# Two tiles of a depthwise convolution as block Toeplitz products on TensorE, and kept weights without their high halves, in a two-layer decoder trunk in fp32

## The chip, the cores and the metric

The kernel runs on one core of one Trainium2 chip. The metric is the device time of one launch in microseconds (us); lower is better. The engines of the core are TensorE (PE, with its weight loads listed apart as PEld), VectorE (DVE), ScalarE (ACT), GpSimd (POOL) and SyncE (SP). In this kernel SP issues the transfers from DRAM and the writes to it, and POOL issues those that read back what the kernel itself has put into DRAM. Each engine works through its own list of instructions in order, and an instruction that waits holds up all that stand behind it in that list.

## The reference

The input x is 512 positions (SEQ) by 1024 channels (D), fp32. There are two layers. Layer 0 mixes by a state-space group and a stick-breaking attention group, layer 1 by a convolution module; behind each mixer stands a feed-forward part with 4096 hidden values, and after each of the four parts a layer norm of 1.414 x + part.

```python
def conformer_conv(x, w_pw1, b_pw1, w_dw, b_dw, ln_g, ln_b, w_pw2, b_pw2):
    h = x @ w_pw1 + b_pw1
    val, gate = jnp.split(h, 2, axis=-1)
    h = val * jax.nn.sigmoid(gate)
    h = lax.conv_general_dilated(
        h, w_dw[:, None, :], window_strides=(1,), padding=[(CONV_SIZE - 1, 0)],
        dimension_numbers=('NWC', 'WIO', 'NWC'), feature_group_count=CONV_WIDTH) + b_dw
    h = jax.nn.silu(layer_norm(h, ln_g, ln_b))
    return h @ w_pw2 + b_pw2

def sqrelu_mlp(x, w1, b1, w2, b2):
    return jnp.square(jax.nn.relu(x @ w1 + b1)) @ w2 + b2
```

The change lies in the convolution module and in what is prepared for it. There each of the 1024 channels is convolved on its own with 31 taps (CONV_SIZE), over the present position and the 30 before it.

## The kernel before

**Products.** Activations lie with channels on the 128 partitions and the 512 positions along the free axis. A fp32 operand is split into a high part in a shorter format (fp32r) and the low rest; a product is then three passes of TensorE: high by high, high by low, low by high (`gemm`, L219). The split is one copy on ACT and one subtraction on DVE (`split`, L215 and L216). Every engine works in the order of its own list; a scheduler at build time makes those lists from the order in which the program names the work and from estimated times, so that neighbours on one engine may come from different loops.

**Weights** (class, L56). Work on weights comes in units of 128 by 1024 values. A unit is fetched by SP into one of two raw buffers, ACT casts it to the high half (L101), DVE subtracts to get the low half (L102), and both go to one of eight slots. A unit is prepared five (or four) units ahead of its use (`AHEAD`), in the order of one list. Thirty units that belong to layer 1 (the list `later`: 16 for the convolution's input projection, `pw1`; 8 for its output projection, `pw2`; 6 for the start of the second feed-forward part) are prepared during the feed-forward part of layer 0, written to DRAM as both halves (`keep`, L109), and read back by POOL when their turn comes (L88).

**Stages, in the order of time.** The mixer of layer 0 comes first; then its output projection and layer norm; then the feed-forward part of layer 0 in four blocks, each of eight hidden tiles `f` (`ffn1`, L988: product, relu, square, split) and the second product `acf` that adds them to X; then the last block's second product with the layer norm folded in, which also begins the next projection on the first half of the positions (`Tail` and `Lead`, tiles `tlb` and `pl`); then the convolution stage; then its output projection `tld`; the second feed-forward part (`fl`, `f`, `g`, `h`); the end.

**The convolution stage** goes over eight tiles of 128 channels. For tile j, `glu_tile` (L1045) makes the value `pv` and the gate `pg` on PE, the sigmoid `csg` of the gate on ACT, the gated product `hp` on DVE with 30 zeros ahead of it, and the split of `hp` into `hph` and `hpl`. The first `PE_TAPS[0][j]` of the 31 taps go to PE (`taps_pe`, L1065): a tap is a product with a diagonal matrix of that tap's weights, in three passes; the matrices `dh` and `dl` are built by ACT from the identity into six buffers (`DBUFS`). Two more taps open the accumulators `cy` and `cz` on ACT, and the rest are multiply-and-add steps on DVE (`taps_dve`, L1078), which end with the addition of `cz` and of PE's `cv`. The sum `sc` over the eight tiles (`LN.add`, L866) is what the layer norm's mean `mpc` is computed from. In the loop at L1095 tile j+2's gate, tile j+1's taps on PE and tile j's taps on DVE are named in turn. The last two tiles are worked in two halves of 256 positions, with taps on PE by `PE_TAPS[1][j]` for the second half, in the order that a string gives:

```python
PE_TAPS = ((2, 6, 8, 9, 11, 14, 13, 14), (10, 10, 10, 10, 10, 10, 13, 8))
TAIL = "P60 P70 V60 V70 G61 G71 N0 P71 P61 V61 V71 N1".split()
```

P is taps on PE, V taps on DVE, G the gate of a second half, N the layer norm of a half; the first digit is the tile, the second the half.

## Time and profile before

| | us |
|---|---|
| median of three runs | 1217.46 (1216.93 to 1217.9) |
| the profiled execution | 1217.5 |
| its span in the profile | 1215.8 |
| granted TensorE clock, mean over the span | 0.995 |
| PE busy | 1187.4 |
| DVE busy | 786.9 |
| ACT busy | 557.1 |
| POOL busy | 58.2 |

The span runs from the first to the last instruction in the profile; the run's time holds 1.7 us more. Times in the timelines are microseconds from the span's start. A row of a timeline gives the start, the length, the engine, the source line with the operation, output and inputs by the names above, and, in brackets, how long the engine was idle before and which instruction released it. A row of groups gives the count, the summed busy time, the mean in ns, and the idle time before these instructions with what ended it. The convolution stage lies between about 662 us (the first gated product) and 795 us (the start of the output projection); the feed-forward part of layer 0 lies ahead of it, from 317 to 594 us.

### The profile page before, as it was taken

What the parts mean: (1) busy time and instruction counts of PE and PEld (TensorE: products, weight loads), DVE (VectorE), ACT (ScalarE), POOL (GpSimd) and SP (SyncE); (2) the same over time, 40 slices, a digit from 0 to 9 for tenths busy, and PEclk for the clock granted to TensorE, in tenths of its full rate; (3) what the DMA queues carried; (4) which work ended last, traced back from release to release, by engine and by line L of the source; (5) the groups of instructions that cost most, each with busy time, mean ns of one, the idle gap of its engine ahead of it and who ended that gap; (6) DMA issues with size and microseconds to landing.
All of it is one profiled execution on the core that took longest, in us unless ns stands there. A gap on an engine that the chain in (4) does not pass through costs nothing.

```text
span 1215.8 us, 16751 instructions
## 1 busy us (share of the span) xinstructions
PE 1187.4 (98%) x6546; PEld 1007.5 (83%) x6546; DVE 786.9 (65%) x1400; ACT 557.1 (46%) x990; POOL 58.2 (5%) x125
## 2 busy tenths in 40 slices
PE   9899999999999999999999999899999999999997
PEld 7677776789988888888999888889988888888885
DVE  7998774578745635646566999998843443434446
ACT  6836665734525524425323456964651332323230
POOL 1001101100000000000022110102000000000000
PEclk9999999999999999999999999999999999999999
DMA  8510042150878787887454631406142232323211
GB/s 205 155 49 22 19 130 61 31 195 1 264 250 282 251 284 264 270 283 268 165 183 159 213 104 36 139 1 208 39 152 87 87 108 83 122 70 121 70 52 69
DMA packets 128943, 168.86 MB, mean 139 GB/s; under 512 B 11298, under 2 KB 101666, under 8 KB 128864
## 3 DMA queue, kind: packets, MB, share of 16 engines
q1 hardware_dynamic: 120064, 136.30, 34.5%
q0 software_dynamic: 8640, 31.46, 7.6%
q8 instruction: 51, 0.84, 0.3%
q14 instruction: 28, 0.23, 0.1%
q10 hardware_dynamic: 160, 0.03, 0.0%
HBM read 132.12 MB, written 35.65 MB: 138 GB/s over the span
## 4 chain that ended last, share of the span: by engine, by line
PE 83%; DVE 10%; ACT 4%; DMA 2%; issue 1%; POOL 0%; SPq 0%; DVEq 0%; POOLq 0%; ACTq 0%
PE f L225 23%; PE g L1175 12%; PE acf L225 11%; PE fl L225 5%; PE tld L225 4%; PE tlb L225 4%; PE h L1159 3%; PE cv L1076 2%; PE pv L225 2%; PE pg L225 2%; PE tla L225 2%; PE pl L225 2%; DVE cz L357 1%; PE acmo L225 1%; PE av L709 1%
## 5 line engine op out<-in xcount | busy, mean ns | idle before, releaser
L102 DVE TENSOR_TENSOR wlo<-raw,whi 128x1024 fp32r<-128x1024 f32 x176 | 213.4, 1224 | 199.5 <-ACT whi L101 198.7
L101 ACT CAST whi<-raw 128x1024 fp32r<-128x1024 f32 x176 | 182.1, 1049 | 313.5 <-PE g L1175 107.4
L1175 PE MATMUL g<-whi,hh 128*128 128x512 f32 x208 | 81.8, 393 | 0.0
L1175 PE MATMUL g<-wlo,hh 128*128 128x512 f32 x208 | 81.8, 393 | 0.0
L1175 PE MATMUL g<-whi,hl 128*128 128x512 f32 x208 | 81.7, 393 | 0.0
L225 PE MATMUL f<-xah,whi 128*128 128x512 f32 x208 | 81.2, 390 | 0.0
L225 PE MATMUL f<-xdl,whi 128*128 128x512 f32 x208 | 81.1, 390 | 0.0
L225 PE MATMUL f<-xah,wlo 128*128 128x512 f32 x208 | 81.0, 390 | 0.0
L225 PE MATMUL f<-xdh,whi 128*128 128x512 f32 x208 | 81.0, 390 | 0.0
L225 PE MATMUL f<-xal,whi 128*128 128x512 f32 x208 | 81.0, 390 | 0.0
L225 PE MATMUL f<-xdh,wlo 128*128 128x512 f32 x208 | 81.0, 390 | 0.0
L225 PE MATMUL acf<-hl,whi 128*128 128x512 f32 x192 | 75.7, 394 | 0.0
L225 PE MATMUL acf<-hh,wlo 128*128 128x512 f32 x192 | 75.6, 394 | 0.0
L225 PE MATMUL acf<-hh,whi 128*128 128x512 f32 x192 | 75.5, 393 | 0.0
L215 ACT CAST hh<-fr 128x512 fp32r<-128x512 f32 x64 | 39.7, 621 | 59.6 <-DVE fr L353 59.6
L216 DVE TENSOR_TENSOR hl<-fr,hh 128x512 fp32r<-128x512 f32 x64 | 44.1, 690 | 31.9 <-ACT hh L215 31.8
L357 DVE SCALAR_TENSOR_TENSOR cy<-hp,wdw,cy 128x512 f32<-128x512 f32 (+1 forms) x99 | 63.6, 654 | 0.2
L357 DVE SCALAR_TENSOR_TENSOR cz<-hp,wdw,cz 128x512 f32<-128x512 f32 (+1 forms) x93 | 60.0, 656 | 0.0
L353 DVE TENSOR_TENSOR fr<-fr 128x512 f32<-128x512 f32 x64 | 43.7, 685 | 14.7 <-ACT fr L154 14.6
L1175 PEld LDWEIGHTS g<-wlo,hh 128*128 128x128 f32 x208 | 39.1, 188 | 8.9
L1175 PEld LDWEIGHTS g<-whi,hl 128*128 128x128 f32 x208 | 39.1, 188 | 8.9
L1175 PEld LDWEIGHTS g<-whi,hh 128*128 128x128 f32 x208 | 39.1, 188 | 8.8
(684 smaller groups left out, 3093.4 us busy)
## 6 DMA issues: line engine op xcount, KB each, us to landing
raw<-in_ffn_w_dram SPq DMA_DIRECT2D x48, 1024.0 KB, 5.8
raw<-in_ffn_w_dram SPq DMA_DIRECT2D x32, 512.0 KB, 3.5
kepth<-whi SPq DMA_DIRECT2D x30, 512.0 KB, 8.6
keptl<-wlo SPq DMA_DIRECT2D x30, 512.0 KB, 9.4
whi<-kepth POOLq DMA_DIRECT2D x30, 512.0 KB, 3.7
wlo<-keptl POOLq DMA_DIRECT2D x30, 512.0 KB, 4.5
raw<-in_conv_w_pw_dram SPq DMA_DIRECT2D x12, 1024.0 KB, 6.5
raw<-in_mix_w_in_dram SPq DMA_DIRECT2D x16, 512.0 KB, 3.9
```

The costliest lines, as they stand in the source:

```text
L101: i0 = nc.scalar.copy(hi, raw).ins
L102: i1 = nc.vector.tensor_sub(lo, raw, hi.bitcast(F32)).ins
L215: i0 = S.copy(hi, src).ins
L216: i1 = V.tensor_sub(lo, src, hi.bitcast(F32)).ins
L225: ins = PE.matmul(ps[:, c0:c1], u[:, k, ksl], v[:, c0:c1], start=start and k == 0 and i == 0, stop=stop and k == n - 1 and i == 2).ins
L353: V.tensor_tensor(o, x, y, op=op)
L357: V.scalar_tensor_tensor(o, x, s, y, op0=op0, op1=op1)
L709: ins = PE.matmul(av[R, P * kb :], vt[:, kb, R], ws_[f"{c}{h}"][0][:, o : o + T - P * kb], start=summed[h] == 1, stop=summed[h] == 4, skip ...
L1076: PE.matmul(cps[j][:, c0:c1], u, v[:, t + c0 : t + c1], start=t == 0 and i == 0, stop=t == n - 1 and i == 2)
L1159: PE.matmul(ps, u, v, start=k == 0 and i == 0, stop=k == nk - 1 and i == 2)
L1175: PE.matmul(pss[b], u, v[:, kk, :], start=k + kk == 0 and i == 0, stop=k + kk == nb - 1 and i == 2)
```

## The change

**Two tiles as Toeplitz products.** Tiles 2 and 3 (`ON_PE`) do their 31 taps on PE alone, in another layout. The 512 positions are taken as four phases (position modulo 4) of 128, and a group of 32 channels with its four phases fills the 128 partitions. An output phase at one shift of whole steps of four positions is then a product with a 128 by 128 matrix that mixes the four phases of a channel. Nine shifts (`SHIFTS`) cover the 31 taps, and there are four groups, so that a tile takes 36 matrices. Each is used in two products (`toeplitz`): the high matrix by the high and the low input side by side, 256 columns, and the low matrix by the high input, 128 columns. `away` adds the two column halves.

The gated product of these tiles is written by phase on DVE (`by_phase`), sent to DRAM and read back in the new layout, then split (`split_phases`); the result goes to DRAM and back (`away`), and ACT puts it into the old order with the bias (`back`). The matrices are made in the feed-forward part of layer 0 (`matrices`): small gathers from a padded copy of the taps, and 36 products of 128 by 512 with a mask on DVE, each written to DRAM by SP. In the convolution stage they are read by POOL into four of the eight weight slots (`M`).

**Kept weights.** Of the thirty kept units only the first four (`BOTH`) are stored as both halves. Of the other 26 the low half is stored; the unit is fetched again by SP and cast again by ACT for the high half, and the low half is read by POOL. The first twenty kept units use four slots only.

**Order and split of taps.** Tiles 1, 4, 5, 6 and 7 have fewer taps on PE for full width and first halves, and tile 7 one fewer in its second half. The order of the first six tiles is written as a string (`CONV_ORDER`: g gate, p taps on PE, v a third of a tile's taps on DVE, s split, m Toeplitz products, o and f the way back, x the scaling of X), and TAIL is another. The buffers of the diagonal matrices go from six to three, the taps are read in the first block rather than ahead of the second, and all additions of `LN.add` are on DVE.

The core of the diff ("..." where lines are left out):

```diff
-PE_TAPS = ((2, 6, 8, 9, 11, 14, 13, 14), (10, 10, 10, 10, 10, 10, 13, 8))
-TAIL = "P60 P70 V60 V70 G61 G71 N0 P71 P61 V61 V71 N1".split()
-DBUFS = 6
+PE_TAPS = ((2, 2, 8, 9, 3, 12, 10, 4), (10, 10, 10, 10, 10, 10, 13, 7))
+TAIL = "G61 P70 P60 V60 V70 G71 N0 P71 P61 V61 V71 N1".split()
+DBUFS = 3
...
+ON_PE = (2, 3)
+SHIFTS = 9
+GROUP = 32
+PARTS = 3
+BOTH = 4
+PAIRS = 1
+CONV_ORDER = "g0 g1 p0 v0 g2 s2 p1 v0 v1 g3 v1 v0 v1 x0 g4 m2 s3 p4 v4 v4 g5 v4 o2 m3 o3 g6 v5 p5 v5 f3 g7 v5 f2".split()
...
+            elif back:
+                i0 = i1 = nc.scalar.copy(hi, raw).ins
+                nc.gpsimd.dma_start(lo, self.kept[back[0]][1])
...
-        for x, d in zip(w, self.kept[i]):
+        for x, d in zip(w, self.kept[i]) if i < BOTH else ((w[1], self.kept[i][1]),):
             self.nc.sync.dma_start(d, x.bitcast(F32))
...
+            if layer == 0 and m >= 8:
+                next(making, None)
...
+    def matrices(i):
...
+        for p_ in range(4):
+            for g in range(4):
+                nc.sync.dma_start(wr[32 * p_ : 32 * p_ + 32, NU * g : NU * (g + 1)], Wd[32 * g : 32 * g + 32, i, p_ : p_ + NU])
+        V.tensor_copy(wh, wr)
+        V.tensor_sub(wl, wr, wh.bitcast(F32))
+        for u in range(0, 4 * NU, 16):
+            for x, src in enumerate((wh.bitcast(F32), wl)):
+                m = tmp(f"m{j}{x}{u}", F32R)
+                V.tensor_tensor(m.rearrange("p (u c) -> p u c", c=GROUP), src[:, u : u + 16].unsqueeze(2).broadcast_to([P, 16, GROUP]),
+                                mask.unsqueeze(1).broadcast_to([P, 16, GROUP]), op=ALU.mult)
+                nc.sync.dma_start(made[j][x][:, u * GROUP : (u + 16) * GROUP], m.bitcast(F32))
+            yield
...
+    def by_phase(j, vps, sg):
...
+        stt(hp[:, :, 8:], ph(vps), pv("conv_b_pw1", j), ph(sg), ALU.add, ALU.mult)
+        Hd = tc.dram_tile([P, 4, P + 8], F32, name=f"Hd{j}")
+        nc.sync.dma_start(Hd, hp)
...
+        for p_ in range(4):
+            nc.sync.dma_start(hps[j][32 * p_ : 32 * p_ + 32], hv[p_])
...
+    def toeplitz(j):
...
+        for g in range(4):
+            o = cps[j][g // 2][:, (g % 2) * 2 * P : (g % 2 + 1) * 2 * P]
+            for e in range(SHIFTS):
+                n = SHIFTS * g + e
+                if n % 8 == 0:
+                    w = M.next()
+                mh, ml = (x[:, n % 8] for x in w)
+                PE.matmul(o, mh, h2[:, :, g, e : e + P], start=e == 0, stop=False)
+                PE.matmul(o[:, :P], ml, h2[:, 0, g, e : e + P], start=False, stop=e == SHIFTS - 1)
+
+    def away(j):
...
+            S.copy(q, z[:, :, 1])
+            tt(r[:, 2 * i * P : (2 * i + 2) * P].rearrange("r (g m) -> r g m", g=2), z[:, :, 0], q, ALU.add)
...
+        nc.sync.dma_start(Od, r.rearrange("r (g m) -> r g m", g=4))
...
+        for g in range(4):
+            nc.sync.dma_start(zv[32 * g : 32 * g + 32], ov[g])
...
-    glu_tile(0)
-    glu_tile(1)
-    taps_pe(0)
-    for j in range(n):
...
+    for o in CONV_ORDER:
```

**How the instructions move, at three places.** The first is ACT's list around the sigmoid of tile 2, `csg` with 512 columns, which the gated product of tile 2 on DVE needs. Before, a diagonal build, the copy for tile 1 (`hph`) and an opened accumulator (`cy`) stand ahead of it:

```order
L154 ACTIVATE dh_6404<-ident,wdh 128x128
L154 ACTIVATE dl_6405<-ident,wdl 128x128
L215 CAST hph_6266<-hp_6265 128x542
L154 ACTIVATE cy_6568<-hp_6265,PV,wdw 128x512
L160 ACTIVATE csg_6362<-pg_6310,PV 128x512
```

Now:

```order
L174 ACTIVATE dl_6863<-ident,wdl 128x128
L235 CAST hph_6406<-hp_6405 128x542
L174 ACTIVATE cy_6555<-hp_6405,PV,wdw 128x512
L174 ACTIVATE cz_6430<-hp_6395,wdw 128x512
L117 CAST whi_6452<-raw_6450 128x1024
L117 CAST whi_6458<-raw_6456 128x1024
L180 ACTIVATE csg_6517<-pg_6467,PV 128x512
```

Two casts of weights (`whi`, for later gates) and one more opened accumulator stand ahead of the sigmoid.

The second place is DVE's list at the end of the convolution stage, where the last addition to `sc` completes the first half's sum (`sc` with 256 columns), and the gated products of the second halves are made (`hp` with 256 columns). Before:

```order
L357 SCALAR_TENSOR_TENSOR hp_6948<-pv_6946,PV,csg_7504 128x256
L353 TENSOR_TENSOR cy_7434<-cy_7434,cz_7435 128x256
L357 SCALAR_TENSOR_TENSOR hp_7140<-pv_7138,PV,csg_7557 128x256
L353 TENSOR_TENSOR cy_7434<-cy_7434,cv_7312 128x256
L216 TENSOR_TENSOR hpl_6950<-hp_6948,hph_6949 128x256
L871 TENSOR_TENSOR sc_6605<-sc_6605,cy_7434 128x256
L216 TENSOR_TENSOR hpl_7142<-hp_7140,hph_7141 128x256
```

Now:

```order
L377 SCALAR_TENSOR_TENSOR cy_7531<-hp_7278,wdw,cy_7531 128x256
L377 SCALAR_TENSOR_TENSOR hp_7278<-pv_7276,PV,csg_7611 128x256
L373 TENSOR_TENSOR cy_7531<-cy_7531,cz_7532 128x256
L373 TENSOR_TENSOR cy_7531<-cy_7531,cv_7405 128x256
L236 TENSOR_TENSOR hpl_7280<-hp_7278,hph_7279 128x256
L373 TENSOR_TENSOR sc_6671<-sc_6671,cy_7531 128x256
```

Tile 6's gated product is earlier in the list, and the low split of tile 7's second half (`hpl_7280`) now stands ahead of the last addition to `sc`, not behind it.

The third is DVE's list at the end of the second block `f` of the feed-forward part of layer 0: `fr` is the square of a hidden tile, `hl` its low split, `X` the first addition of the second product, and `wlo` the low half of a weight unit. Before:

```order
L353 TENSOR_TENSOR fr_4112<-fr_4112 128x512
L102 TENSOR_TENSOR wlo_4208<-raw_4205,whi_4207 128x1024
L102 TENSOR_TENSOR wlo_4238<-raw_4205,whi_4237 128x1024
L216 TENSOR_TENSOR hl_4116<-fr_4112,hh_4115 128x512
L102 TENSOR_TENSOR wlo_4176<-raw_4165,whi_4175 128x1024
L353 TENSOR_TENSOR fr_4150<-fr_4150 128x512
L216 TENSOR_TENSOR hl_4154<-fr_4150,hh_4153 128x512
L353 TENSOR_TENSOR X_61<-X_61,acf_4179 128x512
```

Now:

```order
L373 TENSOR_TENSOR fr_4178<-fr_4178 128x512
L1092 TENSOR_TENSOR m_4188<-w_3891,mask 128x512
L236 TENSOR_TENSOR hl_4182<-fr_4178,hh_4181 128x512
L121 TENSOR_TENSOR wlo_4239<-raw_4236,whi_4238 128x1024
L1092 TENSOR_TENSOR m_4245<-w4h_3892,mask 128x512
L1092 TENSOR_TENSOR m_4248<-w_3891,mask 128x512
L373 TENSOR_TENSOR fr_4222<-fr_4222 128x512
L121 TENSOR_TENSOR wlo_4252<-raw_4236,whi_4251 128x1024
L236 TENSOR_TENSOR hl_4226<-fr_4222,hh_4225 128x512
L373 TENSOR_TENSOR X_61<-X_61,acf_4255 128x512
```

Mask products (`m`) stand among the squares and splits of the hidden tiles, two of them ahead of the last square.

More of the change, by code (lines that the diff above doesn't have):

```diff
@@ L67, in fetch @@
     def fetch(self, i):
[L68 removed]
+        key, src, nk, ncol, off, width, *back = self.units[i]
         if key not in self.chunk:
@@ L832 @@
         if layer:
-            units += [(("split", i), None, 8, 128, 0, 0) for i in range(24 + LEAD)]
+            units += [((f"{u[0][0]}b", *u[0][1:]), *u[1:], i) for i, u in enumerate(later)]
         k0 = 0
@@ L991, in ffn1 @@
             m = k0 + i
+            if then and i == len(first):
+                then()
             if i < len(first):
@@ L1037 @@
         k0 += nb
+    for _ in making:
+        pass
     xs, first = tail_norm_lead(hs, "b", rb[1], ("ln2_g", 0), ("ln2_b", 0), 4, "pl")
+    M.slots = [W.slots[(W.base + 4 + i) % 8] for i in range(4)]
     acc = [None] * KT
@@ L1065, in taps_pe, with back @@
+    def back(j):
+        acc[j] = page(f"cy{j}", F32), None
+        y, zv = acc[j][0].rearrange("c (n q) -> c q n", q=4), cps[j].rearrange("c (q m) -> c q m", q=4)
+        for q in range(4):
+            act(y[:, 3 - q], zv[:, q], AF.Identity, bias=pv("conv_b_dw", j))
     def taps_pe(j, c0=0, c1=T):
```

152 lines of the change are left out of this document (111 added, 41 removed).

## Prediction, made before the changed kernel was run

> **What bounds the kernel now.** I read the page first: the span, and how busy each engine is in it.
>
> ```profile
> span 1215.8 us, 16751 instructions
> PE 1187.4 (98%) x6546; PEld 1007.5 (83%) x6546; DVE 786.9 (65%) x1400; ACT 557.1 (46%) x990; POOL 58.2 (5%) x125
> ```
>
> TensorE (PE) is busy for 98% of 1215.8 us, so it bounds the whole. The one stage where that share misleads is the one changed. The next view gives busy time by stretch of the conv stage (us, PE busy (number of instructions), PEld, DVE, ACT, POOL, granted clock, DMA share, GB/s).
>
> ```profile
> 667.00:700.00 33.00, 33.00 (x146) 27.14 (x146) 32.84 (x52) 14.72 (x37) 5.31 (x10) 1.00 0.62 215
> 700.00:741.00 41.00, 41.00 (x201) 34.50 (x201) 40.51 (x68) 24.87 (x63) 4.22 (x8) 1.00 0.31 103
> 741.00:760.00 19.00, 19.00 (x121) 17.13 (x120) 18.64 (x33) 11.86 (x36) 0.00 (x0) 1.00 0.01 2
> 760.00:783.00 23.00, 18.95 (x156) 18.64 (x154) 23.00 (x55) 21.07 (x65) 4.22 (x8) 1.00 0.54 181
> 783.00:795.00 12.00, 10.30 (x54) 8.84 (x53) 11.62 (x33) 11.20 (x32) 0.00 (x0) 0.86 0.02 6
> ```
>
> VectorE (DVE) is full from 667 to 783 while PE idles for 4 us in the last stretch: two engines run at the edge together, and DVE ends later. The timelines show where (start, length in us, idle before in brackets): first DVE, then PE.
>
> ```profile
> 662.78 0.75 DVE L357 SCALAR_TENSOR_TENSOR hp<-pl,PV,csg 128x512 f32<-128x512 f32 x1 [1.93 <-ACT csg L160]
> 664.24 0.72 DVE L216 TENSOR_TENSOR hpl<-hp,hph 128x542 fp32r<-128x542 f32 x1 [0.71 <-ACT hph L215]
> ...
> 680.83 0.75 DVE L357 SCALAR_TENSOR_TENSOR hp<-pv,PV,csg 128x512 f32<-128x512 f32 x1
> 681.49 0.74 DVE L357 SCALAR_TENSOR_TENSOR cy<-hp,wdw,cy 128x512 f32<-128x512 f32 x1
> ...
> 702.71 0.68 DVE L353 TENSOR_TENSOR cy<-cy,cv 128x512 f32<-128x512 f32 x1
> 703.31 0.74 DVE L357 SCALAR_TENSOR_TENSOR cz<-hp,wdw,cz 128x512 f32<-128x512 f32 x1
> ...
> 778.25 0.50 DVE L357 SCALAR_TENSOR_TENSOR cy<-hp,wdw,cy 128x256 f32<-128x256 f32 x1
> 778.65 0.50 DVE L357 SCALAR_TENSOR_TENSOR cz<-hp,wdw,cz 128x256 f32<-128x256 f32 x1
> ...
> 782.80 0.44 DVE L871 TENSOR_TENSOR sc<-sc,cy 128x256 f32<-128x256 f32 x1
> 783.14 0.44 DVE L216 TENSOR_TENSOR hpl<-hp,hph 128x256 fp32r<-128x256 f32 x1
> ```
>
> ```profile
> 778.36 0.28 PE L225 MATMUL pg<-xbl,whi 128*128 128x256 f32 x1
> 778.48 0.28 PE L225 MATMUL pg<-xbh,wlo 128*128 128x256 f32 x1
> 782.81 0.39 PE L1076 MATMUL cv<-hph,dh 128*128 128x256 f32 x1 [4.05 <-ACT hph L215]
> 783.30 1.22 PE L879 MATMUL mpc<-sc,ones 128*128 128x256 f32 x2
> ```
>
> Durations overlap, so I price by the distance of starts: a 512-wide tap 0.66 us (680.83 to 681.49, both of that operation), a 256-wide tap 0.40, a 512-wide add 0.60 (702.71 to 703.31), a 256-wide add 0.34. The stage on DVE runs from tile 0's gated product (662.78) to the last add of the mean's sum (782.80 + 0.34 = 783.14), 120.4 us; its listed work at these prices is 118.1 (by the order of instructions 130 x 0.66 + 37 x 0.40 + 12 x 0.60 + 18 x 0.34, and 4.2 for splits), so 2.3 are waits. The mean's product (783.30) follows at once, and the output projection starts 12.3 us after the sum:
>
> ```profile
> 655.23 12.00 PE pl L225 x96
> ...
> 700.22 5.49 PE pv L225 x24
> ...
> 795.48 5.46 PE tld L225 x42
> ```
>
> This chain gives PE's prices: 12.00/96 = 0.125 us for a 256-wide product (0.12 between the starts at 778.36 and 778.48 above; I take 0.12), 5.49/24 = 0.229 for a 512-wide one.
>
> **The change, part by part.** *PE.* Removed are 31 full-width taps (tiles 1 to 5: 4+8+9+8+2) of three products, 31 x 3 x 0.229 = 21.3 us, and 14 half-width ones, 14 x 3 x 0.12 = 5.0. Added are 144 Toeplitz products, 72 of 256 columns and 72 of 128, each with its own weight load. A 256-wide product costs 0.12. For 128 columns the trace has few rows (attention scores, 64 rows deep):
>
> ```profile
> 119.38 0.22 PE L672 MATMUL z1B<-qh,kh 64*128 64x128 f32 x1
> 119.44 0.27 PE L672 MATMUL z1B<-ql,kh 64*128 64x128 f32 x1
> 119.55 0.27 PE L672 MATMUL z1B<-qh,kl 64*128 64x128 f32 x1
> ```
>
> Starts lie 0.06 and 0.11 us apart. Bounds of a pair are thus 0.18 and 0.24; I take 0.24, since every product here is behind a load of its own as in the second gap: 72 x 0.24 = 17.3 us. PE's sum: 17.3 - 26.3 = -9.0, of which -8.6 lie ahead of the mean (one half tap of tile 7 comes later). With 0.18 it would be -13.3.
>
> The Trainium skill's "TensorE: Matmul & The Clock Gate" (Back-to-back issue gap) gives about 81 ns per matmul for 128 columns in a stream of load and product. By it a pair is 0.20 and PE's sum -11.9; the rows above hold both readings.
>
> *DVE, conv stage.* Between the same two points the changed list holds 103 instead of 130 operations of 512 (27 x 0.66 = -17.9 us), 50 instead of 37 of 256 taps (+5.2), four 512-wide adds fewer (-2.4) and four 256-wide ones more (+1.4); splits are equal in number. Sum -13.7: with the old waits the sum would end at 769.4. The strided gated product of tiles 2 and 3 is priced as the plain one.
>
> *New waits there.* ACT's builds of diagonal weights (dh), copies, casts and sigmoids cost this much:
>
> ```profile
> L154 ACT ACTIVATE dh<-ident,wdh 128x128 fp32r<-128x128 f32 x98 | 38.3, 391 | 9.2 <-PE cv L1076 6.3 <-DVE wdh L1027 2.8
> L215 ACT CAST hph<-hp 128x542 fp32r<-128x542 f32 x6 | 3.8, 638 | 1.7 <-DVE hp L357 1.7
> L101 ACT CAST whi<-raw 128x1024 fp32r<-128x1024 f32 x176 | 182.1, 1049 | 313.5 <-PE g L1175 107.4 <-PE f L225 65.7 <-PE acf L225 65.2
> 679.58 0.69 ACT L160 ACTIVATE csg<-pg,PV 128x512 f32<-128x512 f32 x1 [8.65 <-PE pg L225]
> 778.80 0.47 ACT L160 ACTIVATE csg<-pg,PV 128x256 f32<-128x256 f32 x1 [0.27 <-PE pg L225]
> 779.29 1.28 ACT L156 ACT_TABLE_LOAD   x1
> ```
>
> (a) Tile 2's sigmoid stands behind two 1.05 us casts, and the second reuses the slot of the gate weights that PE has just finished: 679.6 + 1.05 + 0.69 = 681.3, while DVE, which met the same product at 680.8 and now has two taps (1.3 us) fewer ahead of it, arrives at about 679.5: 2 us of waiting, and every tap behind it in DVE's queue waits too. (b) For tiles 0, 4 and 6 the low split now stands directly behind the gated product, so that DVE waits for ACT's 0.64 us copy: three waits of 0.7, of which one is in today's list (664.24), so 1.4 more. (c) Tile 5's second accumulator opens on ACT behind diagonal weights at 0.39 each, two or three of which DVE's other work does not cover: 1.0. (d) Tile 3's way back through DRAM:
>
> ```profile
> kepth<-whi SPq DMA_DIRECT2D x30, 512.0 KB, 8.6
> Ud<-ue SPq DMA_DIRECT2D x4, 256.0 KB, 2.3
> U<-Ud SPq DMA_DIRECT2D x16, 64.0 KB, 4.4
> ```
>
> A round trip of the same kind lands after 2.3 + 4.4 = 6.7 us; started at 741 it is back at 748, where DVE comes 0.6 earlier; the way out (hp2 done at 682, split needed at 691) is just covered. (e) The second-half sigmoids of tiles 6 and 7 stand behind casts, which DVE's queue covers but for about half of one: 0.6. (f) At the end tile 7's gate (PE at 770), cast 1.05, sigmoid 0.47, table load 1.28 and the high copy 0.4 precede a low split that now stands ahead of the sum: 1.8. Together 7.4 against 2.3 today, +5.1. The sum then ends at 774.8, 8.3 us earlier. PE agrees: its list reaches the end of tile 7's gate at 778.6 - 8.6 = 770.0, and (f)'s chain of about 4 us follows. The normalization after it is unchanged, so the projection starts 8.3 earlier.
>
> *Behind the projection's start* PE is full again. Six more tap products were moved behind it: +0.7. Four casts stand in ACT's queue ahead of the second half's squares; the first is due 14.5 us after the start and done at about 14.7: +0.2. Low halves by DMA cost nothing: they land while PE works on older slots.
>
> *First feed-forward.* 36 mask products of 512, 0.60 each by the add's price, 21.6 us on DVE, 16 in each of the blocks f:
>
> ```profile
> 373.00:417.00 44.00, 44.00 (x200) 36.48 (x201) 27.89 (x35) 25.86 (x40) 0.00 (x0) 1.00 0.83 283
> ```
>
> 27.9 + 9.6 = 37.5 of 44 us: covered by PE's 44, as long as the last hidden tile of a block is split in the 7 x 3 x 0.229 = 4.8 us before PE needs it. Two mask products and a weight split now stand ahead of it. Lower bound 0; upper: 1 to 4 us at each of three block ends, 12. I take 1.0. The DMA there writes 13.6 MB less (26 high halves) and 9.4 MB more (matrices).
>
> **Sum:** -8.3 + 0.7 + 0.2 + 1.0 = -6.4, so 1209.4 for the span; the profiled execution took 1217.5, 1.7 more than its span, at the median of 1217.46. Forecast **1211.1 us**.
>
> The same page of the Trainium skill (Part 1) halves PE's clock after about 3.4 us idle. The trace agrees: 4.05 us idle, then a granted clock of 0.86 in that stretch. If the wait gets shorter than that, the products behind it gain about 1 us, which I leave out.
>
> **Rivals.** *1: the waits don't come up.* For it: they rest on order and rows of a us. Then DVE gains 13.7 and PE, 8.6 plus some 3 of the 4.05 idle, is the bound: -11.6 + 0.7 = 1206.6; with pairs at 0.18 DVE's 13.7 decides: 1204.5. *2: the Toeplitz data are late.* POOL's queue loads matrices and low halves in order, and a matrix slot waits for PE; 4 to 6 us more before tile 2's or 3's last pairs go straight into the sum: about 1216. Against it: POOL is 5% busy. *3: slower, by the first feed-forward.* A mask product waits in DVE's queue until an older one has been written out; kept halves land after 8.6 us there, DMA being at 0.83. If DVE's 6.5 us of room per block are used up, squares and splits behind it are late, and PE waits at three block ends and for weights. From 9 us lost in all it decides; 16 waiting products at 0.8 us give 13: 1211.1 + 12 = 1223. Against it: eight pages rotate. *4: it isn't what it says:* a moving operand of two pieces streams as 512 columns would, 72 x 0.11 = +7.9: 1219. Against it: taps at odd offsets stream at full rate.
>
> **Chances.** Forecast 0.57, rival 1 0.19, rival 2 0.12, rival 3 0.07, rival 4 0.05. The range 1203.5 to 1217.5 holds rivals 1 and 2 and leaves out 3 and 4, and tails. A measurement tells about 0.2% (2.4 us) from no change: faster (below 1215.0) 0.57 + 0.19 + a few of rival 2 = 0.79; same 0.12; slower 0.09.
>
> **What would show it.** Right: the sum's last add near 775, Toeplitz groups near 0.12 us per start, DVE waiting for tile 2's sigmoid and for the last low split, blocks f and acf as long as today. Wrong: PE idle in the first feed-forward; PE waiting for matrices in tile 2 or 3; a Toeplitz tile over 9 us.

## Result: slower by 0.7%, and the profile after

The changed kernel took 1226.12 us (median of four runs, 1223.61 to 1227.69) against 1217.2 us before; the ratio is 1.0071, with a 95% interval of 1.0055 to 1.0087. The profiled execution took 1224.75 us, its span is 1223.0. The forecast was 1211.1 in a range from 1203.5 to 1217.5, and so wrong in its sign.

The page of the changed kernel, its span and the busy times:

```profile
span 1223.0 us, 16822 instructions
PE 1187.4 (97%) x6555; PEld 1007.0 (82%) x6555; DVE 797.3 (65%) x1433; ACT 555.1 (45%) x934; POOL 54.9 (4%) x119
```

PE's busy time is that of before to the tenth, although its list in the convolution stage is shorter: what was saved was spent again on products at a lower clock (the mean granted clock is 0.990, against 0.995 before), and idle time came on top. Where it went is read from the starts on PE's and DVE's timelines, stage by stage. The table holds the two kernels and four of the later runs (us, one profiled execution each; "three acf and tlb" are the stretches from each acf to the next f and from tlb to pl, summed):

| stage | before | changed | e1 | e3 | e4 | e9 |
|---|---|---|---|---|---|---|
| start of the program to first fl | 280.5 | 279.3 | 281.2 | 281.4 | 280.7 | 280.4 |
| first f to first acf | 10.9 | 18.0 | 10.9 | 10.9 | 10.9 | 10.9 |
| three acf and tlb | 182.0 | 185.8 | 186.2 | 181.9 | 183.0 | 182.0 |
| pl to the first gated product | 21.5 | 22.7 | 22.7 | 21.5 | 22.7 | 22.8 |
| first gated product to the sum's last add | 120.0 | 113.6 | 113.7 | 116.9 | 120.4 | 111.9 |
| that add to the output projection | 12.7 | 14.0 | 13.6 | 12.9 | 13.2 | 13.3 |
| output projection to the first g | 104.2 | 105.8 | 106.0 | 104.7 | 104.4 | 105.3 |

The first row is untouched by the change and spreads over 279 to 281 in all executions. The convolution stage gained 3.9 us (21.5 + 120.0 + 12.7 against 22.7 + 113.6 + 14.0), the feed-forward part of layer 0 lost 10.7, the stretch behind the projection 1.6. In all kernels but the changed one the third row holds the transposes of the taps, 0.6 us, so that the block ends of the changed kernel lost 4.5 us and not the 3.8 between the two entries.

Who PE waited for in the feed-forward part, in the changed kernel (total us, times, longest); before the change the same view has no row there:

```profile
PE wd L1063 <- DMA wn<-in_conv_w_dw_dram: 3.0, 2, 1.5
PE acf L245 <- DVE hl L236: 1.8, 2, 1.2
PE tlb L245 <- ACT hh L235: 0.9, 1, 0.9
PE acf L245 <- ACT hh L235: 0.5, 1, 0.5
```

**The first loss** is the transposes of the depthwise taps (`wd`), which the change moved from the start of the second block into the first. First SP's issue of their transfer in the changed kernel, then PE's timeline, then windows ahead of the clock's fall and behind it (length, busy times of the engines, then the granted clock, third from the end):

```profile
315.60 0.79 SPq L1060 DMA_DIRECT2D wn<-in_conv_w_dw_dram  x2
```

```profile
322.69 0.43 PE L1063 MATMUL wd<-ident,wn 31*128 31x31 f32 x4 [1.53 <-DMA wn<-in_conv_w_dw_dram]
323.05 0.50 PE L245 MATMUL f<-xah,wlo 128*128 128x512 f32 x1
...
325.44 0.63 PE L1063 MATMUL wd<-ident,wn 31*128 31x31 f32 x4 [1.42 <-DMA wn<-in_conv_w_dw_dram]
```

```profile
321.37:324.78 3.41, 1.32 (x7) 0.81 (x7) 0.75 (x4) 0.69 (x1) 0.00 (x0) 1.00 0.31 114
324.78:331.61 6.83, 6.17 (x17) 4.95 (x18) 3.23 (x6) 3.32 (x9) 0.00 (x0) 0.50 0.81 251
```

Before, the transfer was issued at 324.3 and the transposes ran at 372.9, 48.6 us later:

```profile
324.26 0.94 SPq L1022 DMA_DIRECT2D wn<-in_conv_w_dw_dram  x2
...
372.90 0.68 PE L1025 MATMUL wd<-ident,wn 31*128 31x31 f32 x8
```

Now there are 7 us between issue and first transpose, PE waits twice, and the granted clock falls to 0.50 behind that, from 324.8 to 331.6 us. The block takes 18.0 us instead of 10.9: 3.0 of waiting, 0.9 for the transposes themselves, and the rest, 3.2, for products at a low clock.

**The second loss** is at the ends of blocks. ACT's timeline ahead of the end of the second block f, then PE's:

```profile
423.00 2.00 ACT L120 CAST whi<-raw 128x1024 fp32r<-128x1024 f32 x2 [0.97 <-DMA raw<-in_conv_w_pw_dram]
424.91 0.67 ACT L174 ACTIVATE fr<-f,PV 128x512 f32<-128x512 f32 x1
427.15 0.62 ACT L235 CAST hh<-fr 128x512 fp32r<-128x512 f32 x1 [1.56 <-DVE fr L373]
```

```profile
427.82 0.50 PE L245 MATMUL acf<-hh,whi 128*128 128x512 f32 x1 [0.54 <-ACT hh L235]
428.90 0.50 PE L245 MATMUL acf<-hl,whi 128*128 128x512 f32 x1 [0.58 <-DVE hl L236]
```

The last hidden tile's relu (`fr`) stands behind two casts that wait for a transfer. Its copy (`hh`) is ready at 427.8 and its low half at 428.9, 6.6 us after acf began (422.25), and PE needs both 4.8 us after that start. Before, the low half of the same tile was done 4.3 us after acf's start at 417.19 (ACT's relu, then DVE's split):

```profile
418.11 0.68 ACT L154 ACTIVATE fr<-f,PV 128x512 f32<-128x512 f32 x1
...
420.76 0.69 DVE L216 TENSOR_TENSOR hl<-fr,hh 128x512 fp32r<-128x512 f32 x1 [0.69 <-ACT hh L215]
```

The relu starts 2.7 us after acf's start instead of 0.9, which is 1.7 of the 2.3 us by which the low half is later; the rest is DVE's list, where mask products and a weight's low half stand ahead of the square and the split. Three block ends lose 1.65, 1.57 and 1.27 us.

**The convolution stage** gained less than forecast. ACT, then DVE, at its start and end:

```profile
670.94 2.00 ACT L117 CAST whi<-raw 128x1024 fp32r<-128x1024 f32 x2 [1.06 <-PE pl L245]
672.84 0.68 ACT L180 ACTIVATE csg<-pl,PV 128x512 f32<-128x512 f32 x1
```

```profile
673.55 0.75 DVE L377 SCALAR_TENSOR_TENSOR hp<-pl,PV,csg 128x512 f32<-128x512 f32 x1 [3.16 <-ACT csg L180]
...
690.60 1.12 DVE L377 SCALAR_TENSOR_TENSOR hp<-pv,PV,csg 128x512 f32<-128x512 f32 x1
691.64 0.75 DVE L377 SCALAR_TENSOR_TENSOR cz<-hp,wdw,cz 128x512 f32<-128x512 f32 x1
...
787.13 0.42 DVE L373 TENSOR_TENSOR sc<-sc,cy 128x256 f32<-128x256 f32 x1
```

The first sigmoid waits for two casts, so the first gated product comes 1.2 us later after the lead (it waits 3.16 instead of 1.93). The gated product by phase takes 1.04 us from start to start, not 0.66. The Toeplitz products themselves cost what was taken for them: 36 pairs from 712.09 to the end of the last product at 720.52, 8.4 us, 0.234 a pair.

```profile
712.09 0.28 PE L1170 MATMUL cv2a<-h,mhi 128*128 128x256 f32 x1
...
720.30 0.22 PE L1171 MATMUL cv2b<-h,mlo 128*128 128x128 f32 x1
```

In tile 3's second half the matrices came late. PE waited twice, 1.29 us in all, its clock fell to 0.50 for the 3.4 us behind that, and the gate of tile 6 that PE makes next was late, so that DVE waited 1.69 us for the sigmoid of it (PE's timeline, a window, DVE's timeline):

```profile
743.24 0.39 PE L1170 MATMUL cv3b<-h,mhi 128*128 128x256 f32 x1 [0.70 <-DMA mhi<-madeh]
744.22 0.33 PE L1171 MATMUL cv3b<-h,mlo 128*128 128x128 f32 x1 [0.59 <-DMA mlo<-madel]
744.62:748.03 3.41, 3.41 (x18) 3.41 (x18) 3.30 (x6) 0.37 (x1) 0.53 (x1) 0.50 1.12 391
753.10 0.48 DVE L377 SCALAR_TENSOR_TENSOR hp<-pv,PV,csg 128x256 f32<-128x256 f32 x1 [1.69 <-ACT csg L180]
```

Behind the sum the granted clock is low for longer than before (0.66 from 783 to 788 there, then 1.00):

```profile
788.00:793.00 5.00, 4.46 (x18) 3.93 (x17) 4.08 (x12) 4.76 (x15) 0.00 (x0) 0.50 0.42 140
793.00:801.10 8.10, 6.14 (x26) 4.81 (x24) 6.87 (x19) 6.97 (x19) 0.00 (x0) 0.83 0.00 0
```

### The profile page after: what moved, and what is told of

The parts are those of the page before. It is cut to its first block, busy times and chain, and to the rows that moved or that the text cites. A ratio compares the mean times of both kernels' runs of the same rounds, so it can differ in the third digit from the quotient of the medians.

```text
span 1223.0 us, 16822 instructions
## 1 busy us (share of the span) xinstructions
PE 1187.4 (97%) x6555; PEld 1007.0 (82%) x6555; DVE 797.3 (65%) x1433; ACT 555.1 (45%) x934; POOL 54.9 (4%) x119
## 4 chain that ended last, share of the span: by engine, by line
PE 65%; DVE 12%; DMA 11%; ACT 6%; issue 4%; POOL 1%; SPq 1%; DVEq 0%; POOLq 0%; ACTq 0%
PE f L245 13%; PE g L1315 12%; PE acf L245 7%; DMA raw<-in_ffn_w_dram 7%; PE tld L245 4%; DVE wlo L121 4%; PE tlb L245 3%; PE h L1299 3%; ACT whi L120 2%; PE pv L245 2%; PE pg L245 2%; DMA raw<-in_conv_w_pw_dram 2%; PE tla L245 2%; PE cv L1206 2%; PE pl L245 2%
## 5 line engine op out<-in xcount | busy, mean ns | idle before, releaser
L377 DVE SCALAR_TENSOR_TENSOR cy<-hp,wdw,cy 128x512 f32<-128x512 f32 (+1 forms) x92 | 57.2, 623 | 0.6
L377 DVE SCALAR_TENSOR_TENSOR cz<-hp,wdw,cz 128x512 f32<-128x512 f32 (+1 forms) x87 | 53.3, 623 | 0.7 <-ACT cz L174 0.4
L245 PEld LDWEIGHTS f<-xah,wlo 128*128 128x128 f32 x208 | 39.7, 191 | 8.4
L245 PEld LDWEIGHTS f<-xah,whi 128*128 128x128 f32 x208 | 39.8, 191 | 8.3
L245 PEld LDWEIGHTS f<-xal,whi 128*128 128x128 f32 x208 | 39.6, 190 | 8.4
```

What stands on the lines that cost most here:

```text
L245: ins = PE.matmul(ps[:, c0:c1], u[:, k, ksl], v[:, c0:c1], start=start and k == 0 and i == 0, stop=stop and k == n - 1 and i == 2).ins
L377: V.scalar_tensor_tensor(o, x, s, y, op0=op0, op1=op1)
```

## Experiments

All were timed together with the kernel before on the same chip; the ratios are to it. There are four groups, each timed on one chip: e1 to e4, e5 to e8, e9 to e11, and e12. The kernel before took 1217.49, 1217.22, 1218.14 and 1217.55 us in them, so that between groups the ratios compare better than the microseconds. Stage times are read as in the table above, where e1 is the first experiment, and so on.

### e1: the taps back at the second block

```diff
-        hs = ffn1(0, bi, k0, nb, xs, nps, first if bi == 0 else (), taps if bi == 0 else None)
+        if bi == 1:
+            taps()
+        hs = ffn1(0, bi, k0, nb, xs, nps, first if bi == 0 else ())
```

> The changed kernel, with one part undone: the depthwise taps are transposed at the start of the second feed-forward block, as before the change, and not in the middle of the first. Theory A (the loss of 7.1 us in the first block f is PE's wait for the taps' transfer, 3.0 us, and the low granted clock behind it): block one takes 10.9 us again instead of 18.0, nothing else moves, and the time falls by 7 us, from 1226 to about 1219. Rival B (the first block is late because its weights are late behind more traffic on SP's queue, and the transposes only stand where PE would have waited anyway): PE waits for weights in the same place and the time falls by 2 us or less, to 1224 or more.

1219.78 us, ratio 1.0023 (0.9999 to 1.0048): 6.3 us less than the changed kernel's 1226.12. The first block is 10.9 again. The block ends lose about as much in all, but elsewhere: nothing at the first, 1.4 and 2.8 us at the other two. Theory A holds on the first block: one transfer issued too close to its use cost some 6 to 7 us, and with it undone the change is within reach of no change at all. The block ends still lose:

```profile
PE acf L245 <- DVE hl L236: 1.2, 1, 1.2
PE tlb L245 <- DVE hl L236: 1.1, 1, 1.1
PE tlb L245 <- ACT hh L235: 1.1, 2, 0.9
```

### e2: mask products into the second products

```diff
-            if layer == 0 and m >= 8:
-                next(making, None)
...
+    def after_sum(bi, k0, j):
+        for _ in range(0 if bi == 0 else 2 if bi == 2 and j % 4 == 3 else 1):
+            next(making, None)
+        return keep_at.get(("a", k0, j), ())
...
-keep=lambda j: keep_at.get(("a", k0, j), ()))
+keep=lambda j: after_sum(bi, k0, j))
```

> As the run before, and also the 36 mask products moved from the blocks f, where DVE was busy 28 of 44 us before the change, into the second products acf, where it was busy 19 to 20 of 44. Theory A (the 4.5 us lost at three block ends come from mask products ahead of the last hidden tile in DVE's list): the blocks acf and tlb take 44.3, 44.6 and 48.1 us again, and the time falls by another 4 to 4.5 us, to about 1214.5. Rival B (the last hidden tile is late because the weights arrive late: the transfers of the matrices lie on the same queue and the casts on ACT and the subtractions on DVE ahead of the hidden tile wait for them): moving the mask products leaves 2 us or more of the loss, and the time is 1216.5 or more.

1216.75 us, ratio 0.9998 (0.998 to 1.0016). The three acf and tlb sum to 183.5: the third acf lost nothing, tlb still 1.6 (49.7 against 48.1). Theory A gave too much to the mask products, rival B too little. The executions spread from 1210.6 to 1222.4, more than those of the kernel before that were timed with it (1214.8 to 1221.4 in 23 runs), so that one profile says little about how often a block end is lost.

### e3: both halves kept

```diff
-BOTH = 4
+BOTH = 30
```

(on top of e1)

> As the first run (taps late), and also all thirty kept units stored and read back as both halves, so that no unit is fetched and cast again. Theory A (ACT's casts ahead of the sigmoids cost 1.2 us at the first gated product, about 1.2 at tile 6 and 1.0 at the last gate, and the casts behind the stage 1.0): DVE's stretch from the first gated product to the last addition of the mean's sum shrinks from 113.9 to about 112, the start of the stage and the stretch behind it by 1 each, and the feed-forward part stays within 1 us: the time falls by 3 to 4 us against the first run, to about 1215.5. Rival B (13.6 MB more written in the feed-forward part, on top of the matrices, makes its weights late): the blocks there grow by 3 us or more and the time is 1219 or more.

1214.29 us, ratio 0.9978 (0.9964 to 0.9993): faster than before, and 5.5 less than e1, more than either theory said. The stage starts at 21.5 after pl again, and no block end is lost, though the mask products stand in the blocks f and 13.6 MB more are written: rival B is wrong. At the end of the third block f casts stand ahead of the last relu on ACT in e1 and in e3. In e1 (first line) the cast waited 4.0 us for its transfer, and the relu came 2.1 us after acf's start at 505.72. In e3 (second line) the transfer had landed, and the relu came 0.2 us after acf's start at 505.88. The order cost time only where the transfer was late:

```profile
506.89 1.05 ACT L120 CAST whi<-raw 128x1024 fp32r<-128x1024 f32 x1 [4.00 <-DMA raw<-in_conv_w_pw_dram]
502.80 2.00 ACT L120 CAST whi<-raw 128x1024 fp32r<-128x1024 f32 x2
```

The stage from the first gated product to the sum got longer, 116.9 against 113.7: DVE now waited in it for Toeplitz data (1.2 us for a split of phases, 1.4 for the way back) and 1.4 for PE, whose taps waited for diagonal matrices. POOL's queue carries 26 more high halves there.

### e4: the kept weights alone

The kernel before, with the changed class for weights and its line of units, and BOTH = 4.

> The kernel before, with the change to the kept weights alone: 26 of 30 units store the low half only, are fetched and cast again, and the first twenty use four slots; the convolution stage is the old one, with no mask products and no matrices. Theory A (the casts ahead of the sigmoids hold up DVE, which is the later engine there, and the feed-forward part gains nothing from writing less because PE covers it): slower by 2 to 5 us, 1219.5 to 1222.5, with the feed-forward part of layer 0 as before within 0.5. Rival B (less traffic, and the casts lie in ACT's idle time): within 1 us of before, 1216.5 to 1218.5.

1221.33 us, ratio 1.0035 (1.0022 to 1.0049): 3.8 us slower, as theory A had it, although not all in the convolution stage: 1.2 at the stage's start, 0.4 in DVE's stretch, 0.5 behind the sum, and 1.1 at tlb, where A expected nothing. ACT at the stage's start shows the same two casts as in the changed kernel:

```profile
662.64 2.00 ACT L111 CAST whi<-raw 128x1024 fp32r<-128x1024 f32 x2 [1.07 <-PE pl L239]
664.54 0.68 ACT L174 ACTIVATE csg<-pl,PV 128x512 f32<-128x512 f32 x1
```

So with the old convolution stage the kept weights alone cost 3.8 us, and by e3 the rest of the change, with the taps where they were, gains 3.2 (1217.49 to 1214.29).

### e5: eight units with both halves

(on top of e2)

```diff
-BOTH = 4
+BOTH = set(range(8))
-            if back and back[0] < BOTH:
+            if back and back[0] in BOTH:
-        for x, d in zip(w, self.kept[i]) if i < BOTH else ((w[1], self.kept[i][1]),):
+        for x, d in zip(w, self.kept[i]) if i in BOTH else ((w[1], self.kept[i][1]),):
```

> As the second run (taps late, mask products in the second products), and the first eight kept units, not four, stored as both halves, so that no cast stands ahead of the sigmoids of tiles 0 and 1. Theory A (the stage starts 1.24 us late because two casts of 1.05 us stand ahead of the first sigmoid in ACT's list, as in all three kernels with low halves only and not in the one with both): from the second half's lead to the first gated product 21.5 us again instead of 22.7, and the rest of the stage as in the second run, 126.1 us to the start of the output projection: 1.2 us faster than the second run, about 1215.5. Rival B (the stage is paced by PE's gates and a start that is earlier on DVE only turns into a wait for tile 2's gate): the output projection starts no earlier after the lead, and the time is as in the second run, 1216.7.

1213.66 us, ratio 0.9973 (0.9962 to 0.9985): 3.1 less than e2 where A expected 1.2. The 1.23 us at the start came as told (21.51). In the profiled execution another 1.2 came between the sum and the projection (12.8 against 14.0 in e2); there the granted clock is 0.50 for 3.4 us, and not for 10.2 as in e2. The length of that low stretch differs between profiles with like waits (last section). The rest of the difference between the medians is not explained by these two profiles.

### e6: the last casts gone too

```diff
-BOTH = set(range(8))
+BOTH = set(range(8)) | set(range(16, 20))
```

> As the run before, and units 16 to 19 (the first four of the output projection) stored as both halves too, so that no cast stands ahead of the last two sigmoids of the stage either. Theory A (the cast of 1.04 us ahead of the last sigmoid delays the chain sigmoid, table load, copy, low split, which ends the mean's sum): the sum ends 0.8 to 1.0 us earlier than in the run before and the time is about 1214.5. Rival B (DVE's list, not that chain, ends the sum): no difference, 1215.5.

1217.11 us, ratio 1.0004 (0.9992 to 1.0015): 3.4 more than e5. Theory A fails: DVE's stretch is 112.1 against 111.9, because DVE's own list ends there without a gap:

```profile
777.62 0.42 DVE L236 TENSOR_TENSOR hpl<-hp,hph 128x256 fp32r<-128x256 f32 x1
777.96 0.42 DVE L373 TENSOR_TENSOR sc<-sc,cy 128x256 f32<-128x256 f32 x1
```

Rival B is right on that, but not on the time. The profiled execution lost 1.8 us at the third acf and 1.35 between sum and projection against e5; why storing four more high halves should bring that about was not settled.

### e7: mask products back in the blocks f

e6 with e2's edit undone.

> The run before with the mask products put back into the blocks f. Theory A (mask products stand in DVE's list between the weights' low halves; a raw buffer is released later, the next transfer is issued later, ACT's cast waits for it, and the copy of a hidden tile stands behind that cast): the third second product acf and tlb grow by 1.4 and 1.2 us, as between the first and the second run, and the time by 2.6, to about 1217. Rival B (the loss at the block ends comes from what follows in the weights' list, the refetch of the first kept units, and twelve units with both halves mend it as thirty did): the block ends lose less than 0.7 us in all and the time is as in the run before.

1218.07 us, ratio 1.0011 (0.9999 to 1.0022): 1.0 more than e6, between the two theories, and no clear difference, since the two intervals overlap. The third acf lost nothing here, where e6 lost 1.8; tlb lost 7.5, the largest loss at a block end in any of the profiles. ACT, PE, and the windows behind:

```profile
594.94 1.99 ACT L120 CAST whi<-raw 128x1024 fp32r<-128x1024 f32 x2 [4.79 <-DMA raw<-in_ffn_w_dram]
596.84 0.61 ACT L235 CAST hh<-fr 128x512 fp32r<-128x512 f32 x1
...
598.30 0.68 ACT L174 ACTIVATE fr<-f,PV 128x512 f32<-128x512 f32 x1
```

```profile
597.50 0.38 PE L245 MATMUL tlb<-hh,whi 128*128 128x256 f32 x1 [3.41 <-ACT hh L235]
599.03 0.58 PE L245 MATMUL tlb<-hl,whi 128*128 128x256 f32 x1 [1.15 <-DVE hl L236]
```

```profile
600.00:604.00 4.00, 4.00 (x20) 3.82 (x19) 1.87 (x4) 0.62 (x1) 0.00 (x0) 0.50 0.99 320
```

Two casts wait 4.8 us for a transfer, and the copy of a hidden tile whose inputs were ready stands behind them. PE runs dry for 4.6 us, and its clock is 0.50 for 6.8 us (598.0 to 604.8, of which the window shows four): tlb took 55.6 us instead of 48.1.

### e8: two more half taps on PE

```diff
-PE_TAPS = ((2, 2, 8, 9, 3, 12, 10, 4), (10, 10, 10, 10, 10, 10, 13, 7))
+PE_TAPS = ((2, 2, 8, 9, 3, 12, 10, 6), (10, 10, 10, 10, 10, 10, 13, 7))
```

(on top of e6)

> As the sixth run, and tile 7's first half has six taps on PE instead of four. DVE has two taps of 0.40 us less ahead of the mean's sum, PE six products of 0.12 more ahead of the last gate. Theory A (at the end of the stage DVE's list sets the sum, PE has 3.1 us of idle time there): the sum ends 0.4 to 0.8 us earlier, time 1214. Rival B (the chain behind PE's last gate sets it): the sum ends 0.7 later, time 1215.2.

1216.13 us, ratio 0.999 (0.9977 to 1.0003), 1.0 less than e6, which the intervals do not separate. The sum ended 0.6 us later, as rival B said. All the same the projection started 1.8 us earlier, since PE's idle time ahead of the last products was shorter and its clock did not fall:

```profile
778.50 0.39 PE L1211 MATMUL cv<-hph,dh 128*128 128x256 f32 x1 [2.28 <-DVE cz L377]
```

```profile
777.00:782.00 5.00, 2.89 (x16) 2.27 (x16) 4.94 (x16) 4.58 (x12) 0.67 (x2) 1.00 0.75 254
782.00:790.00 8.00, 5.06 (x27) 4.21 (x27) 7.51 (x22) 7.97 (x23) 0.00 (x0) 1.00 0.00 0
```

Neither theory had that in it. The third acf lost 4.1 us in this execution (48.6 instead of 44.5), with no mask product in the blocks f: moving these does not mend the block ends by itself.

### e9: the hidden tile ahead of the casts

(on top of e1; mask products in the blocks f, BOTH = 4)

```diff
+                W.hold = layer == 0 and i == nb - 1
                 gemm(ps, W.next(), slice(0, P), xs, 0, T)
+                W.hold = False
...
-            split(hh, hl, r)
+            done = split(hh, hl, r)
+            if layer == 0:
+                W.fence = done
```

`fence` keeps casts and low halves of later weights behind the split of the hidden tile, on ACT and on DVE; `hold` lets the last hidden tile of a block prepare no further unit.

> The first run (taps late, mask products in the blocks f, four units with both halves), with one order added in the feed-forward part of layer 0: casts and low halves of weights that are prepared from a hidden tile on may not stand ahead of the split of the hidden tile before it on ACT and DVE, and the last hidden tile of a block prepares no further unit ahead of its own split. Mask products stay where they are. Theory A (at a block's end ACT's list has casts ahead of the last hidden tile's copy, the casts wait for a transfer that is late, PE runs dry and its clock falls): the blocks from the first acf to tlb sum to 182 to 183 us instead of 186.2, and the time falls by 3 to 4 us, to about 1216. Rival B (the mask products themselves, or the transfers, make the weights late): PE then waits for weights instead of hidden tiles, and the four blocks still sum to 185 or more; time 1219 or more.

1212.39 us, ratio 0.9947 (0.9933 to 0.996): 7.4 less than e1 (9 by the ratios), more than A's 3 to 4. The three acf and tlb sum to 182.0, the value of before, and no wait of PE above 0.15 us is left between 310 and 660 us. That is 4.2 of the 7.8 us between the two profiled executions. Another 1.7 lie in DVE's stretch, where ACT's and DVE's lists are those of e1: PE waited 1.03 us for the matrices instead of 1.38, its clock did not fall, and DVE did not wait for tile 6's sigmoid. The spread is smaller too (1209.8 to 1213.7 in 6 runs; e1 had 1214.0 to 1223.0), but e10, with the same order, spreads as widely as e5 (8.2 us against 6.8). Mask products and low halves are where the change put them, so neither loses at the block ends by itself; the order of casts and low halves around the hidden tile decides. Whether ACT's order, DVE's or the unit held back was enough alone was not tried. ACT at the end of the last block:

```profile
593.26 0.69 ACT L174 ACTIVATE fr<-f,PV 128x512 f32<-128x512 f32 x1 [3.42 <-PE f L245]
594.71 0.62 ACT L235 CAST hh<-fr 128x512 fp32r<-128x512 f32 x1 [0.76 <-DVE fr L373]
595.24 3.90 ACT L120 CAST whi<-raw 128x1024 fp32r<-128x1024 f32 x4
```

This kernel has the lowest ratio of the study and is faster than both kernels.

### e10 and e11: the same order elsewhere

e10 is e5 with e9's edit, e11 the kernel before with it.

> The fifth run (taps late, mask products in the second products, eight units with both halves) with the same order added. Theory A: the blocks sum to about 182 instead of 183.6, no block end is lost in any execution, so that the spread between executions shrinks too, and the time falls by 1.5 to 2.5 us, to about 1211.5. Rival B (weights late in either case): 1213.5 as in the fifth run.

> The kernel before with the same order added and nothing else. Theory A (in the kernel before, the hidden tile is done 1.2 us or more before PE needs it, so that the order changes nothing): 1217.2, the same blocks within 0.3. Rival B (the kernel before loses at block ends in some executions, and the change has only made it more frequent): 1 to 2 us faster than before.

e10: 1214.39 us, ratio 0.9963 (0.9951 to 0.9976), not the 1211.5 of A and no clear difference from e5; the executions lie between 1208.6 and 1216.8, so that the spread did not shrink as A had it. The block ends are whole (182.3), but in the profiled execution the Toeplitz matrices came late, so that the stage took 116.5 instead of 111.9 on DVE:

```profile
734.79 0.39 PE L1179 MATMUL cv3b<-h,mhi 128*128 128x256 f32 x1 [2.48 <-DMA mhi<-madeh]
```

That is rival 2 of the prediction, at 2.5 + 0.7 us of waiting and 6.8 us of a clock at 0.50 behind it, after which DVE waited 4.4 us for tile 6's sigmoid. In e5, which has the same units on POOL's queue, PE waited 0.96 us there; why it was more here stayed open. e11: 1217.28 us, ratio 0.9992 (0.9982 to 1.0003): the kernel before gains nothing, as A said. Its order around hidden tiles had not been losing; the changed lists made it matter.

### e12: the first sigmoid ahead of the casts

(on top of e9)

```diff
-            W.prep_to(W.got + 2)
+            if self.name != "pl":
+                W.prep_to(W.got + 2)
...
-        split(hh[:, p0 : PAD + c1], hl[:, p0 : PAD + c1], hp[:, p0 : PAD + c1])
+        W.fence = split(hh[:, p0 : PAD + c1], hl[:, p0 : PAD + c1], hp[:, p0 : PAD + c1])
+        if j == 0:
+            W.prep_to(W.got + 2)
+        W.fence = None
```

> The ninth run, with the first casts of the convolution stage placed behind the sigmoid and the copy of tile 0 on ACT instead of ahead of them. Theory A (the 1.24 us between the lead and the first gated product are those casts): 21.5 us instead of 22.75, the wait of the first low split 0.7 instead of 1.25, the rest of the stage within 0.5, and the time falls by 1 to 1.5 us, to about 1211. Rival B (three casts of 1.05 us now stand ahead of tile 1's sigmoid, and PE's list waits for the weights that they make): the gain is lost at tile 1 or 2 and the time stays at 1212.4.

1213.2 us, ratio 0.9964 (0.9952 to 0.9976), no faster than e9. The first gated product came 1.0 us earlier (21.8; one cast stayed ahead), and the stage from pl to the projection took 146.8 instead of 147.9. Neither theory had what followed. In the profiled execution the gain was given back right behind, where the output projection's first 6 us ran at a granted clock of 0.52:

```profile
787.50:793.50 6.00, 6.00 (x29) 6.00 (x30) 6.00 (x18) 6.00 (x17) 0.00 (x0) 0.52 0.01 3
```

## Why the prediction was wrong

The profiled span was forecast at 1209.4 and is 1223.0, 13.6 us more. By the prediction's own steps, of which the first and the third were put at nothing:

- **Left out: the moved taps, 6 to 7 us.** The prediction priced no edit for `taps`. Its call had moved from one block to another, and neither the two transfers on SP's queue nor the eight transposes in PE's list were costed there. The row that would have told it was there to be read: before, 48.6 us lie between issue and use. Shown by e1.
- **Mis-sized: "First feed-forward", taken as 1.0, measured 4.5 at three block ends** (1.65 + 1.57 + 1.27). The place was right ("the last hidden tile is split" late) and so were the bounds (1 to 4 us at each of three ends); the middle was not taken but a value near the lower end. The reason given, mask products in DVE's list, is a part of it at most: e3 and e9 have them in place without a loss, and e6 and e8 lose without them. By e9 it is the order of casts and low halves around the hidden tile that decides, and the rows at the second block's end put most of the delay on ACT, where two casts stand ahead of the relu after a wait for a transfer. How raw buffers, SP's queue and DVE's list share in that transfer's lateness stayed open.
- **Wrong: "Low halves by DMA cost nothing".** By e4 the kept weights alone cost 3.8 us. The casts that the change adds were priced at tiles 2, 6 and 7 and behind the projection, but not at the first sigmoid of the stage, which costs 1.2 (e3, e4, e5).
- **Mis-sized: DVE's stretch, forecast 8.3 us shorter, measured 6.4.** The forecast's own terms give 8.6 (13.7 less 5.1); it also took the low split's old wait of 0.7 off with the 2.3, though that wait stays. Neither decides. Waits of 4.6 us were found, against the 7.4 taken, and 1.7 of them were not in the list: the one for tile 6's sigmoid, which came from late matrices and the low clock behind them. (a), taken as 2.0, cost nothing, since DVE arrived with the sigmoid. (f), taken as 1.8, cost 0.12, and e6 shows that DVE's list ends as late without its cast. The listed work was put too low: busy time fell by 10.4 us (118.2 to 107.8), not 13.7; the two products by phase account for 0.8 of the gap, additions that follow one another on the same tile (0.73 apart at 717.83 and 718.56 instead of 0.60) for some more. In e9, without the late gate, the stretch is 8.1 us shorter: close to the forecast, but by luck, since waits put too high and work put too low cancel.
- **Right: the price of the Toeplitz products.** 0.234 us a pair against 0.24; rival 4 is out. Rival 2, late data, came true in a small way: 1.3 us of waiting in tile 3's second half, 1.7 in the sum, against its price of 4 to 6.
- **Left out: the clock behind the stage's idle time.** The prediction named it as a possible gain of 1 us. It went the other way, 12.7 to 14.0 from sum to projection, although PE's wait there got shorter (3.12 against 4.05), and in e12 into the projection itself.
- **Behind the projection:** 0.9 forecast, 1.6 measured.

Of the rivals the third, slower by the first feed-forward, at 1223 in the text with a chance of 0.07, lies nearest the measured time. PE did wait at three block ends, as it said, but not by the mechanism that it named: no mask product was seen to wait for an older one to be written. That its number is near is luck, since about half of the 13.6 us are the taps, which it does not hold. The forecast's mechanism does work where its cover holds: with the taps back and the hidden tile first (e9), the same Toeplitz products, low halves and mask products take 1212.39 us.

## What to carry to other kernels

When a change moves a call, price everything in it on the engine that it lands on, and look up how far its transfer's issue stood ahead of its use before. On an engine that works through its list in order, ask of every instruction that may wait for a transfer what stands behind it; here an order that put the hidden tile ahead of the casts gave back 4.2 us at the block ends, more than the 3.9 that the changed convolution stage gained. A gain or loss of 1 or 2 us next to idle time on PE should be checked against the granted clock before it is explained.

## What was not expected of the hardware

Two waits of 1.53 and 1.42 us with 1.3 us of work between them were enough for the granted clock to fall to 0.50 for 6.8 us (the windows under the first loss). One wait of 2.28 us in e8 left it at 1.00, and one of 3.12 us in the changed kernel brought 0.50 behind it. The waits for tile 3's matrices show how narrow the border can be: 1.29 to 1.74 us in all were followed by 3.4 us at 0.50 (changed, e1, e7, e8), 0.96 to 1.19 us were not (e2, e5, e6, e9, e12). Between the first microseconds and the last, the low stretches of all profiles last 3.4, 6.8 or 10.2 us. The Trainium skill's "TensorE: Matmul & The Clock Gate" (Part 1, The HAM clock gate) speaks of an idle window of about 3.4 us that runs freely, so that the point at which the clock changes differs from run to run. The second half agrees: after idle times of 3.1 us the clock stayed at 0.50 for 10.2 us in the changed kernel, 6.8 in e9 and 3.4 in e5 and e12, and the way from the sum to the projection took 14.0, 13.3, 12.8 and 12.2 us. The first half does not hold for the taps if it means a window without any work: PE was busy for 1.32 of the 3.41 us ahead of the fall.

A pair of a 256-column and a 128-column product, each with a weight load of its own, takes 0.23 us. Within a pair the starts lie 0.17 us apart (712.50 and 712.67), from one pair to the next 0.06 (712.67 and 712.73), so that the price of one of the two cannot be read by itself.
